# Turning the first rows inside the last group of a projection

## The chip, the cores and the metric

The kernel runs on one core of one Trainium2 chip. The metric is the device time of one execution in microseconds: three runs of the kernel before took 1815.97, 1819.52 and 1818.56 us, median 1818.56. Engines are called as the profile calls them: PE (matmuls), PEld (the loads of a matmul's stationary operand), DVE (vector), ACT (activations), POOL (GpSimd), SP (its queue issues most DMAs).

## The reference

One step of a decoder layer, for two groups that share weights. The prompt group has 1024 rows of width 1024, the sample group 8 rows with a paged cache of 8192 positions each.

```python
# prompt rows xp, for each layer (there is one)
q, k, v, logf, u, z = mixer_inputs(rmsnorm(xp, g_mix), w_in, b_f, g_sgu_v)
xp = xp + merge_heads(fox_prompt(q, k, v, logf), sgu_prompt(u, z, w_s, b_s), g_att_out, g_sgu_out, w_o)
mk, mv = memory_kv(mem_prompt, g_mem, w_ck, w_cv)
xp = xp + cross_attend(rmsnorm(xp, g_cross), mk, mv, w_cq, w_co)   # (softmax(q mk / 16) mv) @ w_co, 4 heads
f, conv = conv_ffn(rmsnorm(xp, g_ffn), zeros, w_up, conv_w, conv_b, w_down)  # silu(gate) * val, conv of width 3
xp = xp + f
# the sample rows go through the same layer, attending to cache_k[page_table], cache_v[page_table], cache_logf[page_table]
# a last rmsnorm follows for both; k, v, logf, mk, mv and the last conv rows are returned too
```

All is float32. Each prompt matmul is made of three: both operands are split in a high part (rounded by ACT) and a low part (the rest, by DVE), and high x high, high x low and low x high are summed.

## The kernel before

**The two streams.** The main stream, `prompt`, works on two halves of 512 rows, as four row tiles of 128 (called 0 to 3). Per half: `merge` of the two head groups, `out_proj` with w_o, `cross`, `out_proj` with w_co at the end of `cross`, and `ffn`. The second stream, `sample`, handles the sample rows: `decode` goes through the cache in steps, of which each gathers a tile of keys (1 MB, a 128x2048 tile, through POOL's queue), multiplies it on DVE (L1423) and sums it on DVE (L1427), and gathers values that go through PE (L1475); later `sample_rest` takes all weights through PE again for eight rows.

**The order.** Both streams are Python generators that yield a cost. The loop at the end of `build` adds the main stream's yields to a credit, and while the credit is at least `PACE` of the phase (8.0 in the first half's middle part, 6.8 in the second's, 8.5 in the first feed-forward, 2.5 in the second, 2.9 once the sample stream is in its rest) it emits a step of the sample stream, at most one or a few per yield. Nothing is emitted while `held[0]` is true; the credit goes on growing. This gives the order of the program; a scheduler then places the instructions on every engine's queue by its own simulated times, an earlier instruction going first where several are ready. [...] Decode's DVE instructions are put behind the newest DVE instruction of the main stream.

**The projections.** `out_proj` computes [512 rows] x [1024 columns] in two halves of the columns. In the first half (L1055 to L1057) all four row tiles go side by side. In the second half (L1073 to L1075) row tiles go in three groups, (0), (1) and (2, 3). A group has eight slices of the contraction, with three matmuls of 512 columns per slice and row tile: 24, 24 and 48. After a group `residual` adds the bank to x (L1007, DVE) and takes the square's sum (L230, ACT). Before a feed-forward, the rows are also scaled by their norm: `factor` (ACT L1023, then a power on POOL, L1024) and `scaled` (ACT L1029) for rows 0 and 1, `both` (L1036, L1037) for rows 2 and 3. Before `cross` this scale is applied later, in the softmax.

**The turn.** `norm_T` transposes the rows (L1106, PE) two row tiles at a time, four steps of two contraction slices each, and splits the result (L238 on ACT, L239 on DVE) into `hs` and `ls`. It then runs the first column tile of the next projection on these 256 columns of rows: 24 matmuls through `gemm3` (L272 to L274). So the first column tile is made in two halves, all others with 512 columns at once. This happens in four places: before `cross` and before `ffn`, in both halves.

**Buffers.** PSUM has four banks tagged `ba`, two `bb`, one `ms` and one `dv`; `BK` (also called `MM` and `TR`) takes `bb` at each third turn. Weights come by `wload`: a DMA into one of 4 `wr` buffers, then `split` into one of 5 `wh` (L235) and one of 4 `wl` (L236). `U` tiles (128x1024 floats, tag `u`) number 18, key and value tiles 4.

Of the kernel before, what the change touches and what calls it, by code (L numbers as in the profile page):

```python
# [30 lines left out]
NF = FF // P  # L31
# [47 lines left out]
def build(nc, tc, ctx, a, phases=None):  # L79
# [70 lines left out]
    MM = TR = BK  # L150
# [847 lines left out]
    held = [False]  # L998
# [15 lines left out]

    def out_proj(w, mh, ml, xt, fetch=None, ys=None):

        sq = squares()
# [9 lines left out]
        def scaled(i, r):  # L1027
            y = U([P, D])
            nc.scalar.activation(y, xt[i], AF.Copy, scale=r)  # L1029
            return y  # L1030
# [11 lines left out]
        for n in range(2):  # L1042
# [24 lines left out]
            for group in ((0,), (1,), (2, 3)):  # L1067
                pss = [MM() for _ in group]
                for k in korder:
                    wh, wl = (ws[k // 2][q][:, k % 2, :] for q in range(2))  # L1070
                    for i, ps in zip(group, pss):
                        tb = slice(i * P, (i + 1) * P)
                        mmul(ps, mh[k][:, tb], wh, start=(k == korder[0]), stop=False)  # L1073
                        mmul(ps, mh[k][:, tb], wl, start=False, stop=False)
# [14 lines left out]

    def norm_T(ys, g0, first):  # L1090


        hs, ls = [], []
        for t0 in (0, 2):
            c = slice(t0 * P, (t0 + 2) * P)
            if callable(ys[t0]):
                ys[t0:] = ys[t0]()
            for kk in range(0, 8, 2):
                if t0 == 0:
                    h2, l2 = U([P, 2, 512], F32R), U([P, 2, 512], F32R)  # L1100
                    hs += [h2[:, 0, :], h2[:, 1, :]]
                    ls += [l2[:, 0, :], l2[:, 1, :]]
                tr = TR()
                for q in range(2):
                    for i in range(2):
                        nc.tensor.transpose(  # L1106
                            tr[:, (q * 2 + i) * P : (q * 2 + i + 1) * P], ys[t0 + i][:, (kk + q) * P : (kk + q + 1) * P], ident
                        )
# [11 lines left out]
    def cross(xt, sq):  # L1120
        mkn, mkT, mv, pp, pT = ([None] * MH for _ in range(5))
# [10 lines left out]

        ws = [wload(wpair(a["w_cq"], kk, 0, 512), 1024) for kk in range(4)]
        q2, ps0 = [], MM()

# [108 lines left out]
        ys = []  # L1244
        sq = yield from out_proj(a["w_co"], oh, ol, xt, ys=ys)
        return ys


    hlast = [const.tile([P, 2 * NF, 2], F32, tag=f"hlast{h}", name=f"hlast{h}") for h in range(2)]

    def ffn(hf, xt, ys, late=None):
# [18 lines left out]
        for gi, gn in enumerate(GROUPS):  # L1270
            gh, gl = [], []
            for f in range(f0, f0 + gn):
                hc2 = []
                for part in range(2):
                    ft = f + part * NF
                    cw = [gp[:, CW + i * 44 + ft : CW + i * 44 + ft + 1] for i in range(3)]
                    cb = gp[:, CB + ft : CB + ft + 1]
                    if ft:
                        w_, pv = wload(a["w_up"][ft], 1024), BK()
                        up(pv, w_, hs, ls, slice(0, 512))  # L1280
                    else:
                        pv = pv0
                    hc = T2()
# [547 lines left out]
    def prompt():  # L1831
# [38 lines left out]
        for hf in range(2):  # L1870
# [8 lines left out]
            if ends:  # L1879
                yield from ends.pop()  # L1880
            sq = yield from out_proj(a["w_o"], mh, ml, xt, partial(load_x, hf))
            if hf == 0:
                ys = yield from mix(cross(xt, sq), gating(1), 0.05)
            else:
                ys = yield from cross(xt, sq)
            phase[0] = f"ffn{hf}"
            sq = yield from ffn(hf, xt, ys, (lambda: ahead.append(merge(*merge_in(1))) or ahead[0]) if hf == 0 else None)
            held[0] = False
# [123 lines left out]
```

## Time and profile before

| what | value |
|---|---|
| runs | 1815.97, 1819.52, 1818.56 us (median 1818.56) |
| profiled execution | 1820.56 us, of which the span of the program 1818.4 us |
| granted PE clock over the span | 0.986 |
| busy: PE / DVE / ACT / POOL | 1745.0 / 1397.5 / 734.4 / 510.0 us |
| moved by DMA | 521.06 MB, mean 287 GB/s |
| the four turns | 547.6 to 569, 706.6 to 727, 1182.6 to 1201, 1350.8 to 1364 us |

In the timeline a row has the start, the duration, engine, line, operation, the tiles written and read, the shape, and in brackets the idle time of the engine just before it with what ended it. Matmuls overlap, so what one costs is read from the distance of two starts, not from its duration. The granted clock is the share of full speed that PE had in a stretch.

### The profile page before, as it was taken

How to read it: one execution, taken by the hardware profiler on the slowest of the kernel's cores; microseconds unless marked ns; L12 is line 12 of the kernel's file. 1: busy time of each engine (PE TensorE's matmuls, PEld its weight loads, DVE VectorE, ACT ScalarE, POOL GpSimd, SP SyncE). 2: the span in 40 equal slices, each digit the busy share in tenths (PEclk: the TensorE clock that was granted, in tenths of full speed). 3: DMA queues.
4: the chain of work that ended last, by engine and by line, in shares of the span. 5: the costliest groups of instructions: out<-in, count | busy, mean ns of one | idle time of the engine just before them, and what ended most of it. 6: DMA issues, size and time to landing. Idle time of an engine off the chain costs nothing.

```text
span 1818.4 us, 25090 instructions
## 1 busy us (share of the span) xinstructions
PE 1745.0 (96%) x9637; PEld 1294.9 (71%) x9637; DVE 1397.5 (77%) x1729; ACT 734.4 (40%) x1378; POOL 510.0 (28%) x461
## 2 busy tenths in 40 slices
PE   8999999888998999999999999989899999999997
PEld 5887776656676767777777776766576778767775
DVE  4689668888788877999989899898875549845344
ACT  6332365455643544433333244235353324332332
POOL 1252334332133432223332333334222111011110
PEclk9999999899999999999999999989999999999999
DMA  8886889777696986679878779988787777568982
GB/s 295 306 297 231 302 297 329 242 266 224 219 398 257 342 310 260 257 285 340 316 279 311 271 306 340 381 300 324 290 309 290 267 268 265 179 266 289 359 314 82
DMA packets 157074, 521.06 MB, mean 287 GB/s; under 512 B 20874, under 2 KB 40842, under 8 KB 124186
## 3 DMA queue, kind: packets, MB, share of 16 engines
q0 software_dynamic: 57168, 341.14, 49.5%
q1 hardware_dynamic: 92874, 165.73, 26.4%
q10 hardware_dynamic: 6912, 12.59, 1.8%
q8 instruction: 76, 1.25, 0.3%
q14 instruction: 44, 0.36, 0.1%
HBM read 495.47 MB, written 23.93 MB: 286 GB/s over the span
## 4 chain that ended last, share of the span: by engine, by line
PE 72%; DMA 10%; issue 7%; DVE 6%; ACT 2%; POOL 2%; SPq 0%; POOLq 0%; DVEq 0%; ACTq 0%
PE ba L272 11%; PE ba L274 11%; PE ba L273 11%; PE bb L272 5%; PE bb L273 5%; PE bb L274 5%; PE dv L1475 5%; DMA kv<-cache_k,io 3%; DMA wr<-w_in 2%; DMA kv<-cache_v,io 1%; PE dv L321 1%; PE dv L1751 1%; PE ba L1056 1%; PE ba L1055 1%; PE ba L1057 1%
## 5 line engine op out<-in xcount | busy, mean ns | idle before, releaser
L235 ACT ACTIVATE wh<-wr 128x1024 fp32r<-128x1024 f32 (+2 forms) x220 | 228.9, 1044 | 489.2 <-PE ba L273 156.0
L236 DVE TENSOR_TENSOR wl<-wr,wh 128x1024 fp32r<-128x1024 f32 (+2 forms) x220 | 262.5, 1200 | 175.6 <-PE ba L274 65.7
L1407 POOL DMA_INDIRECT kv<-cache_k,io x128 | 205.6, 1606 | 551.2 <-DVE s L1427 318.9
L1423 DVE TENSOR_TENSOR kv<-kv,d 128x1024 f32<-128x1024 f32 (+1 forms) x156 | 258.0, 1681 | 35.1 <-DMA kv<-cache_k,io 35.1
L1427 DVE TENSOR_REDUCE s<-kv 128x16 f32<-128x1024 f32 (+1 forms) x156 | 258.2, 1674 | 0.1
L1469 POOL DMA_INDIRECT kv<-cache_v,io x128 | 165.3, 1291 | 282.8 <-PE dv L1475 191.8
L272 PE MATMUL ba<-u,wh 128*128 128x512 f32 (+1 forms) x560 | 220.3, 395 | 1.7 <-ACT u L238 1.7
L273 PE MATMUL ba<-u,wh 128*128 128x512 f32 (+1 forms) x560 | 220.2, 393 | 1.7 <-DVE u L239 1.5
L274 PE MATMUL ba<-u,wl 128*128 128x512 f32 (+1 forms) x560 | 219.5, 393 | 0.0
L272 PE MATMUL ba<-wh,u 128*128 128x512 f32 (+1 forms) x495 | 186.9, 379 | 0.9 <-ACT u L235 0.9
L273 PE MATMUL ba<-wl,u 128*128 128x512 f32 (+1 forms) x495 | 185.4, 375 | 1.2 <-DVE wl L236 1.2
L274 PE MATMUL ba<-wh,u 128*128 128x512 f32 (+1 forms) x495 | 183.8, 376 | 0.0
L272 PEld LDWEIGHTS ba<-u,wh 128*128 128x128 f32 x560 | 106.8, 191 | 30.6 <-issue 5.6
L273 PE MATMUL bb<-u,wh 128*128 128x512 f32 (+1 forms) x304 | 119.4, 393 | 9.2 <-DVE u L239 9.2
L274 PEld LDWEIGHTS ba<-u,wl 128*128 128x128 f32 x560 | 106.9, 191 | 29.1 <-issue 6.1
L273 PEld LDWEIGHTS ba<-u,wh 128*128 128x128 f32 x560 | 106.7, 191 | 27.5 <-issue 2.7
L1475 PE MATMUL dv<-kv,s 128*32 128x512 f32 x1024 | 124.2, 598 | 1.8 <-DMA kv<-cache_v,io 1.8
L272 PE MATMUL bb<-u,wh 128*128 128x512 f32 (+1 forms) x304 | 119.4, 393 | 0.0
L274 PE MATMUL bb<-u,wl 128*128 128x512 f32 (+1 forms) x304 | 118.6, 390 | 0.0
L272 PEld LDWEIGHTS ba<-wh,u 128*128 128x128 f32 x495 | 93.0, 188 | 26.0 <-issue 6.9
L274 PEld LDWEIGHTS ba<-wh,u 128*128 128x128 f32 x495 | 92.8, 188 | 21.5 <-issue 3.7
L273 PEld LDWEIGHTS ba<-wl,u 128*128 128x128 f32 x495 | 93.1, 188 | 19.7 <-DVE wl L236 1.9
(425 smaller groups left out, 3255.9 us busy)
## 6 DMA issues: line engine op xcount, KB each, us to landing
wr<-w_up SPq DMA_DIRECT2D x88, 512.0 KB
kv<-w_up POOLq DMA_DIRECT2D x22, 1024.0 KB, 8.0
wr<-w_down SPq DMA_DIRECT2D x40, 512.0 KB
kv<-w_down POOLq DMA_DIRECT2D x11, 1024.0 KB, 8.5
wr<-w_in SPq DMA_DIRECT2D x16, 512.0 KB
wr<-w_o SPq DMA_DIRECT2D x16, 512.0 KB
wr<-w_cq SPq DMA_DIRECT2D x16, 512.0 KB
wr<-w_co SPq DMA_DIRECT2D x16, 512.0 KB
```

Source lines behind the costliest of these rows:

```text
L235: nc.scalar.activation(h, src, AF.Copy)
L236: nc.vector.tensor_tensor(l, src, h.bitcast(F32), op=ALU.subtract)
L272: mmul(out, sh, mh, start=(i == 0), stop=False)
L273: mmul(out, sh, ml, start=False, stop=False)
L274: mmul(out, sl, mh, start=False, stop=(i == n - 1))
L321: mmul(ps[32 * j : 32 * j + 32, :w], xT[:, k, :] if nk == 8 else xT[:, k * 8 : k * 8 + 32], raw[:, q, j * w : (j + 1) * w], start=(k == 0) ...
L1055: mmul(pss[i], mh[k][:, tb], wh, start=(k == korder[0]), stop=False)
L1407: nc.gpsimd.indirect_dma_start(kv, None, a["cache_k"], off(kidx[:, b, ch : ch + 1]))
L1423: nc.vector.tensor_tensor(kvv[:, i : i + m, :], kvv[:, i : i + m, :], qb.unsqueeze(1).broadcast_to((P, m, 512)), op=ALU.mult)
L1427: nc.vector.tensor_reduce(s[:, ch * 4 + i : ch * 4 + i + m, :].rearrange("p k h -> p (k h)"), kvv[:, i : i + m, :].rearrange("p k (h d) -> ...
L1469: nc.gpsimd.indirect_dma_start(kv, None, a["cache_v"], off(kidx[:, b, ch : ch + 1]))
L1475: mmul(dv[32 * j : 32 * j + 32, :], s[:, ch * 4 : ch * 4 + 4, :].rearrange("p k h -> p (k h)"), kvv[:, j, :], start=(ch == 1), stop=(ch == ...
```

## The change

The transposes of rows 0 and 1 move into the last group of `out_proj`, the one of row tiles 2 and 3. `norm_T` now returns a generator `turn` with the two lists; `ahead_of` makes `hooks` from it, a table from slice number to what is to be emitted behind that slice: the loads of the weights of the next projection behind slices 0-based 1, 3, 5 (and 7 for the four w_cq loads), and the four steps of `turn(0)` behind slices 2, 3, 5, 6 before `cross` and 3, 4, 5, 6 before `ffn`. Row 1's scaling is emitted behind slice 1 of the group, where it was emitted behind the group.

`halves` follows the group: three banks of `ba` are taken, three column tiles run on columns 0 to 255 (rows 0 and 1), then `turn(2)` transposes rows 2 and 3, then the three tiles run on columns 256 to 511. In `cross` these are column tiles 0, 1, 2 of w_cq; in `ffn` the tiles 0, 22 and 1 of w_up. The loops that follow take these banks instead of computing the tiles.

`held[0]` becomes true at the start of the last group, where it became true at its end, and stays so until `halves` is done. The group's two banks, and those of the transposes of rows 2 and 3, are `bb`; the transposes of rows 0 and 1 use `ba`.

```diff
@@ out_proj, second half of the columns
             for group in ((0,), (1,), (2, 3)):
-                pss = [MM() for _ in group]
-                for k in korder:
+                held[0] = len(group) == 2
+                pss = [BB() if held[0] else MM() for _ in group]
+                for at, k in enumerate(korder):
...
-                    if len(group) == 2 and k == korder[3]:
-                        yield 5.2
-                if ys is not None and group[0]:
-                    ys.append(scaled(group[0] - 1, factor(group[0] - 1)))
+                    if len(group) == 2:
+                        if ys is not None and at == 1:
+                            ys.append(scaled(1, factor(1)))
+                        for hook in hooks.get(at, ()):
+                            hook()
+                        if at == 3:
+                            yield 5.2
+                if ys is not None and group[0] == 1:
+                    ys.append(scaled(0, factor(0)))
                 for i, ps in zip(group, pss):
                     residual(xt, sq, i, n, ps)
-
-                held[0] = len(group) == 2
                 yield 5.2
@@ norm_T: the body of the loop over rows becomes turn(t0)
-                tr = TR()
+                tr = BB() if t0 else BA()
...
-            first(hs, ls, c)
-            if t0 == 0:
-                yield 3
+
+        return hs, ls, turn
+
+    def ahead_of(turn, loads, at):
+
+        steps = turn(0)
+        hooks = {k: [partial(next, steps)] for k in at}
+        ws = []
+        for n, load in enumerate(loads):
+            hooks.setdefault(1 + 2 * n, []).insert(0, lambda load=load: ws.append(load()))
+        return hooks, ws
+
+    def halves(products, turn):
+
+        banks_ = [BA() for _ in range(3)]
+        for c in (slice(0, 256), slice(256, 512)):
+            if c.start:
+                for t in turn(2):
+                    yield t
+            for d, ps in enumerate(banks_):
+                products(ps[:, c], d, c)
+                yield 2.8
         held[0] = False
-        return hs, ls
+        return banks_
@@ cross
-        ws = [wload(wpair(a["w_cq"], kk, 0, 512), 1024) for kk in range(4)]
-        q2, ps0 = [], MM()
+        q2 = []
...
-        hs, ls = yield from norm_T(xt, G_CROSS, lambda hs, ls, c: products(ps0[:, c], ws, 0, hs, ls, c))
+        begun = yield from halves(lambda out, d, c: products(out, ws, d, hs, ls, c), turn)
...
-                if n or dt_:
+                if n or dt_ > 2:
...
-                    ps = ps0
+                    ps = begun[dt_]
...
+        hs, ls, turn = norm_T(ys, G_FFN)
+        hooks, ws = ahead_of(turn, [partial(wload, a["w_up"][ft], 1024) for ft in (0, NF, 1)], (3, 4, 5, 6))
+        yield from out_proj(a["w_co"], oh, ol, xt, hooks, ys=ys)
+        return hs, ls, turn, ws
@@ ffn
-        w0, pv0 = wload(a["w_up"][0], 1024), BK()
...
-        hs, ls = yield from norm_T(ys, G_FFN, lambda hs, ls, c: up(pv0[:, c], w0, hs, ls, c))
+        begun = yield from halves(lambda out, d, c: up(out, ws[d], hs, ls, c), turn)
+        begun = dict(zip((0, NF, 1), begun))
...
-                    if ft:
+                    pv = begun.pop(ft, None)
+                    if pv is None:
                         w_, pv = wload(a["w_up"][ft], 1024), BK()
                         up(pv, w_, hs, ls, slice(0, 512))
-                    else:
-                        pv = pv0
@@ prompt
+            hs, ls, turn = norm_T(xt, G_CROSS)
+            hooks, ws = ahead_of(turn, [partial(lambda kk: wload(wpair(a["w_cq"], kk, 0, 512), 1024), kk) for kk in range(4)], (2, 3, 5, 6))
+            sq = yield from out_proj(a["w_o"], mh, ml, xt, hooks, partial(load_x, hf))
```

More of the change, by code (lines that the diff above doesn't have):

```diff
@@ L1088, in out_proj, with norm_T, turn @@
         return sq
-    def norm_T(ys, g0, first):
+    def norm_T(ys, g0):
         hs, ls = [], []
-        for t0 in (0, 2):
+        def turn(t0):
             c = slice(t0 * P, (t0 + 2) * P)
@@ L1100, in norm_T @@
                     h2, l2 = U([P, 2, 512], F32R), U([P, 2, 512], F32R)
[L1101 to L1103 removed]
+                    hs.extend([h2[:, 0, :], h2[:, 1, :]])
+                    ls.extend([l2[:, 0, :], l2[:, 1, :]])
+                tr = BB() if t0 else BA()
                 for q in range(2):
@@ L1112, in norm_T, with cross @@
                 yield 0.6
-            first(hs, ls, c)
-            if t0 == 0:
-                yield 3
+        return hs, ls, turn
[15 more added lines that the diff above has]
+                yield 2.8
         held[0] = False
-        return hs, ls
-    def cross(xt, sq):
+        return banks_
+    def cross(xt, sq, hs, ls, turn, ws):
         mkn, mkT, mv, pp, pT = ([None] * MH for _ in range(5))
@@ L1244, in cross, with ffn @@
         ys = []
-        sq = yield from out_proj(a["w_co"], oh, ol, xt, ys=ys)
-        return ys
+        hs, ls, turn = norm_T(ys, G_FFN)
+        hooks, ws = ahead_of(turn, [partial(wload, a["w_up"][ft], 1024) for ft in (0, NF, 1)], (3, 4, 5, 6))
+        yield from out_proj(a["w_co"], oh, ol, xt, hooks, ys=ys)
+        return hs, ls, turn, ws
     hlast = [const.tile([P, 2 * NF, 2], F32, tag=f"hlast{h}", name=f"hlast{h}") for h in range(2)]
-    def ffn(hf, xt, ys, late=None):
-        w0, pv0 = wload(a["w_up"][0], 1024), BK()
+    def ffn(hf, xt, hs, ls, turn, ws, late=None):
         def up(out, w, hs, ls, c):
@@ L1880, in prompt @@
                 yield from ends.pop()
[L1881 to L1885, printed above, removed]
+            hs, ls, turn = norm_T(xt, G_CROSS)
+            hooks, ws = ahead_of(turn, [partial(lambda kk: wload(wpair(a["w_cq"], kk, 0, 512), 1024), kk) for kk in range(4)], (2, 3, 5, 6))
+            sq = yield from out_proj(a["w_o"], mh, ml, xt, hooks, partial(load_x, hf))
+            step = cross(xt, sq, hs, ls, turn, ws)
+            got_ = yield from (step if hf else mix(step, gating(1), 0.05))
             phase[0] = f"ffn{hf}"
-            sq = yield from ffn(hf, xt, ys, (lambda: ahead.append(merge(*merge_in(1))) or ahead[0]) if hf == 0 else None)
+            sq = yield from ffn(hf, xt, *got_, (lambda: ahead.append(merge(*merge_in(1))) or ahead[0]) if hf == 0 else None)
             held[0] = False
```

2 lines of the change are left out of this document (1 added, 1 removed).

## The prediction

> **What bounds the kernel now.** I read the page first, then the stages around the four projection ends, then single engines there.
>
> ```profile
> span 1818.4 us, 25090 instructions
> ...
> PE 1745.0 (96%) x9637; PEld 1294.9 (71%) x9637; DVE 1397.5 (77%) x1729; ACT 734.4 (40%) x1378; POOL 510.0 (28%) x461
> ...
> PE 72%; DMA 10%; issue 7%; DVE 6%; ACT 2%; POOL 2%; SPq 0%; POOLq 0%; DVEq 0%; ACTq 0%
> ```
>
> PE is busy 96% of the span and carries 72% of the chain: time comes only from PE's gaps and its clock. The stages, four of them the places that the diff touches (columns: window, length, busy of PE, PEld, DVE, ACT, POOL, granted clock, DMA share, GB/s):
>
> ```profile
> 548.00:570.00 22.00, 18.82 (x114) 15.20 (x113) 21.20 (x34) 9.38 (x22) 5.38 (x6) 0.84 0.87 330
> 707.00:725.00 18.00, 14.89 (x80) 12.51 (x79) 11.34 (x25) 12.39 (x31) 3.54 (x4) 0.81 0.81 329
> 1183.00:1203.00 20.00, 13.96 (x91) 10.86 (x94) 18.44 (x30) 9.40 (x21) 6.82 (x5) 0.74 0.77 273
> 1351.00:1366.00 15.00, 13.38 (x83) 11.87 (x82) 10.08 (x21) 11.81 (x29) 1.10 (x2) 0.89 0.42 165
> 570.00:590.00 20.00, 18.35 (x104) 13.21 (x106) 13.37 (x19) 6.18 (x8) 8.68 (x3) 1.00 0.51 178
> 725.00:800.00 75.00, 75.00 (x355) 57.16 (x355) 71.62 (x70) 30.46 (x49) 19.50 (x14) 1.00 0.64 237
> 800.00:1100.00 300.00, 300.00 (x1418) 222.36 (x1417) 280.15 (x252) 103.15 (x155) 95.22 (x65) 1.00 0.82 310
> 1250.00:1285.00 35.00, 28.87 (x128) 19.89 (x124) 27.74 (x31) 19.89 (x54) 13.32 (x8) 0.95 0.83 297
> ```
>
> In the first four PE idles and the clock falls; in 725 to 1100 PE never idles. Inside the places (timeline; the last bracket is idle time and its releaser):
>
> ```profile
> 546.20 0.39 PE L1073 MATMUL ba<-wh,u 128*128 128x512 f32 x1
> 546.43 0.39 PE L1074 MATMUL ba<-wl,u 128*128 128x512 f32 x1
> 547.59 1.03 PE L1106 MATMUL ba<-cp,u 128*128 128x128 f32 x8
> 548.46 0.60 PE L1106 MATMUL bb<-cp,u 128*128 128x128 f32 x4
> 552.13 0.28 PE L272 MATMUL bb<-u,wh 128*128 128x256 f32 x1
> 552.25 0.28 PE L273 MATMUL bb<-u,wh 128*128 128x256 f32 x1
> 560.14 0.39 PE L273 MATMUL bb<-u,wh 128*128 128x256 f32 x1 [2.05 <-DVE u L239]
> 563.98 0.58 PE L273 MATMUL bb<-u,wh 128*128 128x256 f32 x1 [0.80 <-DVE u L239]
> 712.01 0.47 PE L1106 MATMUL ba<-cp,u 128*128 128x128 f32 x1 [1.12 <-ACT u L1036]
> 712.98 0.58 PE L272 MATMUL ba<-u,wh 128*128 128x256 f32 x1 [0.50 <-ACT u L238]
> 1193.97 0.58 PE L273 MATMUL bb<-u,wh 128*128 128x256 f32 x1 [5.59 <-DVE u L239]
> 1199.88 0.28 PE L274 MATMUL bb<-u,wl 128*128 128x256 f32 x1
> 1355.29 0.39 PE L272 MATMUL ba<-u,wh 128*128 128x256 f32 x1 [1.04 <-ACT u L238]
> ```
>
> Starts give the real cost of one: 0.23 us for 512 columns, 0.12 for 256, 0.87/8 = 0.109 for a transpose. The gaps wait for the split of transposed rows (L238, L239), and at 1193 DVE was busy elsewhere:
>
> ```profile
> 1191.18 2.35 DVE L1423 TENSOR_TENSOR kv<-kv,d 128x1024 f32<-128x1024 f32 x2
> 1193.44 0.47 DVE L239 SCALAR_TENSOR_TENSOR u<-ba,gp,u 128x256 fp32r<-128x256 f32 x1
> ```
>
> Decode's steps sit ahead of the prompt's split. That is what the earlier hold acts on.
>
> **The prize.** Idle: 3.18 + 3.11 + 6.04 + 1.62 = 13.95 us. Clock: (1 - granted) x length = 3.52 + 3.42 + 5.20 + 1.65 = 13.8. Idle inside slow time is counted twice: in the third place 10.4 us (twice 5.20) ran slow (0.58 at 1193.97), up to the return to 0.28 at 1199.88, so it began near 1189.4 and about 4.5 us of the gap lay in it: 2.2 too many. Half of the 0.80 in the first and of some 1.4 in the second make 1.1 more. 27.7 - 3.3 = **24.4 us** is the most that can go. Since PE has no spare time behind the places, what is saved there reaches the end.
>
> **The change, part by part.**
>
> *Rows 0 and 1 turned inside the last group.* 16 transposes (1.7 us of PE, as before) move between the slices of the 48 matmuls of rows 2 and 3 (48 x 0.23 = 11 us), so their eight splits run under these. Are the rows there? Before a feed-forward, row 1 must pass residual, square, POOL's power and scaling:
>
> ```profile
> 1340.86 0.68 DVE L1007 TENSOR_TENSOR u<-ba,u 128x512 f32<-128x512 f32 x1
> 1344.11 1.16 ACT L1029 ACTIVATE u<-u,fac 128x1024 f32<-128x1024 f32 x1 [0.68 <-POOL fac L1024]
> ```
>
> That takes 4.4 us; the first hook stands behind 4 x 6 x 0.23 = 5.5 us. Covered by 1.1; without it PE, in program order there, would stand for the difference. Cross needs only the residual. PE cost 0.
>
> *Three tiles begun on columns 0 to 255.* 72 half products (8.6 us) stand where 24 stood, so the residuals, scaling and transposes of rows 2 and 3 are hidden by 8.6 instead of 2.9 us. Price: 48 more pairs of halves per place, each 2 x 0.12 - 0.23 = 0.01: 192 x 0.01 = **1.9 us**. [...]
>
> *Rows 2 and 3 turned behind the 72,* in the two BB banks alone. Nothing covers the first split:
>
> ```profile
> 706.65 0.60 PE L1106 MATMUL bb<-cp,u 128*128 128x128 f32 x4
> 707.87 0.36 PE L272 MATMUL ba<-u,wh 128*128 128x256 f32 x1
> 707.28 0.47 ACT L238 ACTIVATE u<-bb,gp 128x256 fp32r<-128x256 f32 x1 [2.14 <-PE bb L1106]
> ```
>
> From transpose to first product 1.22 us, of which eight transposes fill 0.87; the low part (DVE, 0.47 at 1193.44) costs some 0.4 more. 0.8 per place, **3.2 us**. Ends: 0 if the order pulls the transposes forward; 6.5 if each place stays as the best one was (1.62).
>
> *Weights.* The four w_cq or three w_up loads (SP's DMA, ACT's high and DVE's low part) move into the group, in the same order on SP; the four key and value fetches of cross now queue behind the w_cq loads, and are first read after five column tiles (27 us of PE at 24 x 0.23 each). The last w_cq slice's buffer comes free only at the group's end: two residuals (0.68 each) and its low part (wl, 1.22 below) make 2.6 us, wanted after 18 half products, 2.2. **0.9 us** for two cross places; ends 0 and 2.4, where both low parts stand bare.
>
> *The hold.* Decode stops at the group's start: 29.6 units of yields are held (2 x 5.2, 6 x 2.8, 4 x 0.6) in place of 13.0 (5.2, 8 x 0.6, 3), some 32 us of PE work (11 + 3.5 + 144 x 0.12). Work held is not saved: 16.6 more units are owed afterwards, two steps per place, each of two DVE instructions over a 128x2048 tile, and POOL's gathers wait for buffers that these release. On PE decode's matmuls only move. A place's yields grow from 28.6 to 40.0 units in all, so over the whole kernel decode is asked for sooner, and its tail is no new end.
>
> ```profile
> 731.02 2.28 DVE L1423 TENSOR_TENSOR kv<-kv,d 128x2048 f32<-128x2048 f32 x1
> 733.22 1.22 DVE L236 TENSOR_TENSOR wl<-wr,wh 128x1024 fp32r<-128x1024 f32 x1
> 734.36 0.74 DVE L1286 SCALAR_TENSOR_TENSOR t<-ba,gp,t 128x511 f32<-128x511 f32 x1
> 735.02 2.28 DVE L1427 TENSOR_REDUCE s<-kv 128x32 f32<-128x2048 f32 x1
> ```
>
> In the first feed-forward three yields of finished tiles come at once, each with a step of 4.6 us: 13.7 us of DVE while PE has one ready tile, 5.5 us, and a pair of decode's matmuls, 1.9. Weight splits slip between (733.22), so I take **2.5 us**, between 0 and 6.3 (13.7 - 7.4).
>
> *Clock.* Left gaps of 0.8 us: does it still fall?
>
> ```profile
> 588.92 1.50 PE L1475 MATMUL dv<-kv,s 128*32 128x512 f32 x12 [1.65 <-DMA kv<-cache_v,io]
> ```
>
> A lone gap of 1.65 left 570 to 590 at 1.00; a cluster with none above 1.04 cost 1.65 us at 1351. I take one such loss in the four, **1.7**; ends 0 and 6.8. [...]
>
> **Sum.** 24.4 - 1.9 - 3.2 - 0.9 - 2.5 - 1.7 = **14.2 us**. The profiled execution took 1820.56 us (span 1818.4), 2.0 above the runs' median of 1818.56: 1806.4 for it, **1804.4** as a median. All good ends: 24.4 - 1.9 = 22.5, 1796.1. All bad ends: 24.4 - 1.9 - 6.5 - 2.4 - 6.3 - 6.8 = 0.5, 1818.1.
>
> **Rivals.**
>
> *The transposes do not get under the group.* They wait for rows, for banks (BA, four) or for the 18 U buffers (8 for the turned rows, 8 for the projection's input, 4 for x). Then only the wait for rows 2 and 3 is hidden, about half the prize: 12.2 - 1.9 - 3.2 - 2.5 = 4.6, 1814.0. For: the margin of 1.1. Against: each slice frees two U buffers before a hook wants them. Chance 0.13.
>
> *DVE becomes the bound after the release.* In the first feed-forward a tile wants 1.22 + 2 x 0.74 + 0.68 = 3.4 us of DVE, a step 4.6: 8.0 against 6.5 to 7.4 on PE, for 29.6 / (8.5 - 5.2) = 9 tiles. 1.5 x 9 = 13 us if all shows: the gain is 14.2 + 2.5 - 13 = 3.7, 1815. For: DVE is 95% busy (71.62 of 75). Against: the same catch-up over four tiles there cost PE nothing. Chance 0.11.
>
> *Slower: late keys block DVE's queue.* A step released into a full DMA waits at DVE's head with the prompt's splits behind it:
>
> ```profile
> 1275.38 2.36 DVE L1423 TENSOR_TENSOR kv<-kv,d 128x1024 f32<-128x1024 f32 x2 [4.81 <-DMA kv<-cache_k,io]
> 1278.40 2.08 PE L1170 MATMUL bb<-t,u 128*128 128x256 f32 x4 [4.19 <-DVE u L236]
> ```
>
> That cost 4.19 and 0.05 x 35 = 1.75 of clock, 5.9. From the third such new stall on (14.2 / 5.9 = 2.4) the change loses; four make 1828. For: after the hold a step comes every 5.2 units where 6.8 or 8.0 were paced, 2 MB of keys and values in some 5.5 us, 380 GB/s, above the 297 in which this one waited. Against: four key buffers fill during the hold, and 570 to 590 has half the DMA free. Chance 0.16.
>
> **How the numbers follow.** The forecast has 0.60: 1804.4, its own range from the good ends to half of the bad ones, 1796 to 1811. Faster takes the forecast, the first rival and a quarter of the second: 0.76; within 0.2% (3.6 us, about what this kernel's measurement can tell) 0.08; slower 0.16. The range 1795 to 1823 reaches through the second rival into the third.
>
> **What would show it.** Transposes between slices of the last group, their splits done by its end; four windows with clock above 0.95 and under 1.5 us idle; 256-column products three times as many; DVE without decode in them, and in the first feed-forward PE idle below 3 us. It is wrong if the clock still falls in these places, or if new gaps ended by DMA or DVE stand in the 40 us behind a release.

## The result, and the profile after

The changed kernel takes 1828.32 us (median of 9 runs, 1821.75 to 1835.07), the kernel before 1816.06 (9 runs, 1811.78 to 1819.52). The ratio is 1.0061 [1.0044, 1.0078]: about 12 us slower, where 14 us faster was forecast.

The page of the changed kernel, first lines and the chain that ended last:

```profile
span 1821.4 us, 25458 instructions
...
PE 1744.1 (96%) x9829; PEld 1301.8 (71%) x9829; DVE 1397.6 (77%) x1725; ACT 736.3 (40%) x1378; POOL 517.3 (28%) x461
...
PE 41%; issue 15%; DMA 11%; DVE 8%; POOL 5%; ACT 1%; POOLq 0%; DVEq 0%; SPq 0%; ACTq 0%
```

PE is as busy as before (96%), but it carries 41% of the chain instead of 72%; DMA, DVE and POOL, the engines of decode's steps, carry 24% instead of 18%. The stages (columns as in the prediction: window, length, busy of PE, PEld, DVE, ACT, POOL, granted clock, DMA share, GB/s); the first four are the places, the others lie behind them:

```profile
548.00:570.00 22.00, 21.46 (x177) 19.42 (x176) 21.73 (x37) 7.31 (x16) 9.41 (x6) 1.00 0.89 355
707.00:729.00 22.00, 18.63 (x140) 17.89 (x139) 8.76 (x18) 11.26 (x26) 1.08 (x2) 0.92 0.31 108
1202.00:1222.00 20.00, 17.86 (x149) 15.77 (x148) 19.64 (x28) 5.72 (x12) 7.11 (x6) 1.00 0.95 351
1357.00:1375.00 18.00, 17.97 (x147) 17.37 (x146) 6.85 (x14) 9.63 (x21) 1.10 (x2) 1.00 0.43 177
615.00:630.00 15.00, 11.80 (x53) 7.09 (x52) 12.87 (x16) 7.01 (x19) 4.89 (x4) 0.77 1.03 402
...
800.00:900.00 100.00, 99.02 (x472) 72.43 (x472) 92.04 (x80) 34.87 (x52) 41.01 (x23) 1.00 0.86 318
925.00:945.00 20.00, 16.34 (x61) 12.81 (x60) 16.63 (x17) 5.17 (x5) 4.07 (x3) 0.83 0.78 290
1100.00:1151.00 51.00, 45.12 (x227) 31.69 (x226) 45.13 (x52) 19.80 (x37) 17.36 (x16) 1.00 0.98 382
1545.00:1562.00 17.00, 13.59 (x48) 10.57 (x47) 17.00 (x22) 5.36 (x9) 2.16 (x3) 0.80 0.65 219
```

The places are mended: idle there is 0.54 + 3.37 + 2.14 + 0.03 = 6.1 us for 13.95 before, and the clock costs 0.08 x 22 = 1.8 us for 13.8. But in stretches where PE hardly idled before it now waits, with the clock down behind it: 615 to 630, 925 to 945 and 1545 to 1562. From 1100 to 1151 it idles 5.9 us at full clock, in five waits of at most 1.8 us.

What PE waits for (timeline, PE; the last bracket is idle time and its releaser). The first two rows are transposes between slices of the last group, as planned; the row at 707.21 has the 12 transposes that came behind their group; the others are the waits:

```profile
546.32 0.49 PE L1110 MATMUL ba<-cp,u 128*128 128x128 f32 x3
547.81 0.60 PE L1110 MATMUL ba<-cp,u 128*128 128x128 f32 x4
...
620.80 3.64 PE L1497 MATMUL dv<-kv,s 128*32 128x512 f32 x16 [3.20 <-DMA kv<-cache_v,io]
707.21 1.47 PE L1110 MATMUL ba<-cp,u 128*128 128x128 f32 x12
711.92 0.42 PE L272 MATMUL ba<-u,wh 128*128 128x256 f32 x1 [3.25 <-DVE u L239]
933.60 0.39 PE L1482 MATMUL ms<-dg,ones 128*128 128x8 f32 x2 [2.32 <-DVE dg L1475]
935.33 0.80 PE L272 MATMUL ba<-wh,u 128*128 128x512 f32 x1 [1.34 <-DVE u L1341]
1556.18 0.80 PE L274 MATMUL ba<-wh,u 128*128 128x512 f32 x1 [3.41 <-DVE u L236]
```

At 933 and 1556 PE waits for something short on DVE. DVE's own order shows why: at 933 a multiply of decode's keys waits for its gather, and the 0.21 us instruction that PE wants (decode's own softmax), and the prompt's residual sums, stand behind it:

```profile
928.93 2.29 DVE L1445 TENSOR_TENSOR kv<-kv,d 128x2048 f32<-128x2048 f32 x1 [3.37 <-DMA kv<-cache_k,io]
931.14 2.28 DVE L1449 TENSOR_REDUCE s<-kv 128x32 f32<-128x2048 f32 x1
933.34 0.21 DVE L1475 TENSOR_SCALAR dg<-cp,mT 8x8 f32<-8x8 f32 x1
933.47 1.21 DVE L236 TENSOR_TENSOR wl<-wr,wh 128x1024 fp32r<-128x1024 f32 x1
934.60 1.27 DVE L1341 TENSOR_TENSOR u<-ba,u 128x512 f32<-128x512 f32 x2
```

DVE took these in that order: decode's 0.21 us and the prompt's sums, for which PE waits at 933 and at 935, stood 3.37 + 2.29 + 2.28 us behind a key step of decode. At 1556 DVE waits for no transfer at all; it is full with the sample's key steps, two products and two sums of 1.2 us each, ahead of the split (0.68 us) of the last gate product:

```profile
1547.32 2.35 DVE L1679 TENSOR_TENSOR kv<-kv,d 128x1024 f32<-128x1024 f32 x2
...
1552.06 2.33 DVE L1681 TENSOR_REDUCE sS<-kv 128x4 f32<-128x1024 f32 x2
1554.31 1.21 DVE L236 TENSOR_TENSOR wl<-wr,wh 128x1024 fp32r<-128x1024 f32 x1
1555.44 0.68 DVE L236 TENSOR_TENSOR u<-t,u 128x512 fp32r<-128x512 f32 x1
```

By stage (us between starts of matmuls in the trace; the last three columns are experiments told below):

| stage | before | after | after, second profile | turn | credit and turn | and sample |
|---|---|---|---|---|---|---|
| up to the end of w_o, first half | 546.9 | 548.9 | 550.8 | 547.7 | 550.0 | 549.0 |
| place 1, cross-attention, up to w_co | 104.9 | 104.0 | 107.4 | 101.6 | 100.8 | 98.8 |
| w_co | 54.1 | 53.6 | 53.6 | 53.7 | 53.8 | 53.8 |
| place 2, first feed-forward, merge, up to w_o | 429.3 | 444.7 | 446.5 | 441.4 | 427.5 | 426.0 |
| w_o, second half | 46.6 | 49.8 | 49.8 | 50.3 | 50.3 | 50.3 |
| place 3, cross-attention, up to w_co | 113.6 | 97.9 | 97.2 | 97.3 | 102.3 | 103.7 |
| w_co | 54.6 | 58.0 | 58.0 | 55.8 | 56.1 | 56.4 |
| place 4, second feed-forward, to the last matmul | 458.6 | 454.5 | 455.1 | 460.9 | 463.4 | 454.1 |
| last matmul starts at | 1808.7 | 1811.4 | 1818.3 | 1808.7 | 1804.1 | 1792.1 |

(The stages named w_o and w_co now hold the transposes of rows 0 and 1, so some 2 us move into them.) Up to the second half's w_co the gain comes in one stage, place 3, and goes in one, the first feed-forward, 15 us longer. (What place 1 gains, 0.9 us, is less than the 2 us that moved out of it.) Of the 15.7 us at place 3, 3.2 moved into w_o, and some 6 belong to the late key at 1278 that the prediction shows in the kernel before (4.19 us of idle and 1.75 of clock): neither profile of the changed kernel has that wait, and no term of the sum had it. In the first feed-forward the gaps grew from 5.8 to 17.0 us, the slow clock cost 1.7 more, and three key steps more, with 16 value matmuls of 0.12 us, brought 1.9: 14.7 of the 15.4. The profiled execution of before took 4.5 us more than the median of its runs, that of after 5 us less than its; the second profile of after (1830.11 us) stands near its median, and its last matmul starts 9.6 us behind that of before.

### The profile page after: what moved, and what is told of

It reads as the page before. It is cut to its first block, busy times and chain, and to the rows that moved or that the text cites. A ratio compares the mean times of both kernels' runs of the same rounds, so it can differ in the third digit from the quotient of the medians.

```text
span 1821.4 us, 25458 instructions
## 1 busy us (share of the span) xinstructions
PE 1744.1 (96%) x9829; PEld 1301.8 (71%) x9829; DVE 1397.6 (77%) x1725; ACT 736.3 (40%) x1378; POOL 517.3 (28%) x461
## 4 chain that ended last, share of the span: by engine, by line
PE 41%; issue 15%; DMA 11%; DVE 8%; POOL 5%; ACT 1%; POOLq 0%; DVEq 0%; SPq 0%; ACTq 0%
DMA kv<-cache_k,io 5%; PE ba L273 5%; PE ba L274 5%; PE ba L272 5%; PE dv L1497 3%; POOL kv L1429 2%; PE bb L273 2%; PE bb L272 2%; DMA kv<-cache_v,io 2%; PE bb L274 2%; POOL kv L1491 2%; DVE s L1449 2%; DVE kv L1445 1%; DMA u<-an_d 1%; PE dv L321 1%
## 5 line engine op out<-in xcount | busy, mean ns | idle before, releaser
L1491 POOL DMA_INDIRECT kv<-cache_v,io x128 | 178.3, 1393 | 282.0 <-PE dv L1497 198.0
L273 PE MATMUL ba<-u,wh 128*128 128x512 f32 (+1 forms) x656 | 237.6, 366 | 1.4 <-DVE u L239 1.4
L274 PE MATMUL ba<-u,wl 128*128 128x512 f32 (+1 forms) x656 | 236.2, 363 | 0.0
L272 PE MATMUL ba<-u,wh 128*128 128x512 f32 (+1 forms) x656 | 232.0, 364 | 3.4 <-DVE u L239 3.2
L272 PE MATMUL ba<-wh,u 128*128 128x512 f32 (+1 forms) x521 | 199.4, 384 | 3.2 <-DVE u L1341 1.3
L273 PE MATMUL ba<-wl,u 128*128 128x512 f32 (+1 forms) x521 | 197.7, 381 | 2.0 <-DVE wl L236 2.0
L274 PE MATMUL ba<-wh,u 128*128 128x512 f32 (+1 forms) x521 | 194.4, 380 | 4.4 <-DVE u L236 4.4
L273 PEld LDWEIGHTS ba<-u,wh 128*128 128x128 f32 x656 | 123.9, 189 | 32.6 <-issue 9.0
L274 PEld LDWEIGHTS ba<-u,wl 128*128 128x128 f32 x656 | 123.9, 189 | 27.1 <-issue 7.3
L272 PEld LDWEIGHTS ba<-u,wh 128*128 128x128 f32 x656 | 121.3, 189 | 26.7 <-issue 3.5
L272 PEld LDWEIGHTS ba<-wh,u 128*128 128x128 f32 x521 | 99.4, 191 | 29.1 <-issue 5.7
L274 PEld LDWEIGHTS ba<-wh,u 128*128 128x128 f32 x521 | 98.9, 190 | 26.0 <-DVE u L236 5.3
L272 PE MATMUL bb<-u,wh 128*128 128x512 f32 x272 | 108.1, 397 | 0.0
L273 PE MATMUL bb<-u,wh 128*128 128x512 f32 x272 | 107.5, 395 | 0.0
L274 PE MATMUL bb<-u,wl 128*128 128x512 f32 x272 | 107.5, 396 | 0.0
```

What stands on the lines that cost most here:

```text
L272: mmul(out, sh, mh, start=(i == 0), stop=False)
L273: mmul(out, sh, ml, start=False, stop=False)
L274: mmul(out, sl, mh, start=False, stop=(i == n - 1))
L1491: nc.gpsimd.indirect_dma_start(kv, None, a["cache_v"], off(kidx[:, b, ch : ch + 1]))
```

## The experiments

**Decode's steps or the hold.** The first two theories: more of decode's steps fall into the first feed-forward (44 key steps for 41), or the earlier hold itself costs. Four kernels: the change with decode at a slower pace there (41 steps again), before at a faster one (45 steps), the change with the hold where it was, and before with the earlier hold alone.

```diff
-'ffn0': 8.5
+'ffn0': 9.1        # e5_pace91, on the changed kernel
+'ffn0': 7.7        # e6_before_pace77, on the kernel before
```

> The changed kernel with the pace of the first feed-forward at 9.1 instead of 8.5: nothing else. By count of the program, decode then does 41 key steps between w_co's last residual and the feed-forward's end, as the kernel before, where the changed kernel does 44. Theory A (the change pushes three more decode steps, some 14 us of DVE, into a feed-forward in which DVE is already full): that stage falls from 445 us to 425 to 430 and the whole to 1806 to 1814, clearly below the changed kernel's 1828. Theory B (the longer hold itself, by late transfers behind it): stage 440 or more, whole 1823 to 1830.

Measured: 1821.25 us, 1.0028 [1.0009, 1.0048]. Its first feed-forward took 434.6 us, 10 less than the changed kernel's, yet only 7 us came back in all.

> The kernel before with the pace of the first feed-forward at 7.7 instead of 8.5, which makes 45 key steps there of 41 and leaves everything else. Theory A: the stage grows from 429 us to 443 to 450; the second half's middle part gets shorter by some 5, since decode is done sooner; whole 1820 to 1830. Theory B: the stage stays within 4 of 429, whole 1812 to 1819.

Measured: 1813.96 us, 0.9995 [0.9977, 1.0013]. 45 steps cost the kernel before nothing, so the count of steps by itself is not what costs.

```diff
 # e2_late_hold, on the changed kernel
-                held[0] = len(group) == 2          (ahead of the group)
...
+                held[0] = len(group) == 2          (behind its residuals, as before)
```

> The changed kernel with the hold at the end of the last group again (the banks stay bb): 43 key steps in the first feed-forward. Theory A: nearly the changed kernel, 1820 to 1828, the stage 437 to 445. Theory B: most of the loss goes, 1808 to 1817.

Measured: 1828.33 us, 1.0046 [1.0025, 1.0066]: no better.

> The kernel before with the hold from the start of the last group and nothing else: 43 key steps in the first feed-forward of 41, no extra yields. Theory A: two steps more, 9 us of DVE there, part of it seen: 1816 to 1824. Theory B: the whole loss without any of the gain, 1828 to 1840.

Measured: 1816.89 us, 0.9999 [0.9986, 1.0013]. The earlier hold by itself, on the kernel before, costs nothing and brings nothing.

**What the change is worth without the second stream.** Decode and sample left out of both kernels:

```diff
-    bgs.append(sample())
+    bgs.append(iter(()))
```

> The kernel before without the second stream: decode and all that follows for the sample rows behind the input projection is left out, so their outputs are not written. PE's prompt work alone. Base for the next run; 1560 to 1640 (1024 decode matmuls and the sample rows' weights less).

> The changed kernel without the second stream. With DVE free at the places the splits wait less, so the gain should be smaller than the 24 us of idle time and clock: theory C 6 to 16 us below the kernel before without the stream; theory D less than 4 below, or above.

Measured: 1584.63 us (1582.75 to 1586.93) and 1571.58 us (1569.89 to 1574.84). The change gains 13.1 us on the prompt alone. With the second stream it loses 12: some 25 us go in the meeting of the two streams. That 13.1 is near the 14.2 of the forecast is luck. The forecast rests on 24.4 us of idle and slow time in the places, and most of that is made by the second stream: without it the kernel before idles 5.1 us in them (22 us around each) and loses 3.4 to the clock, the changed kernel 0.6 and nothing. That is some 8 of the 13.1 us; where the other 5 come from is not shown.

```diff
 # n_one: n_after with one begun tile
-        banks_ = [BA() for _ in range(3)]
+        banks_ = [BA()]
...
-                if n or dt_ > 2:
+                if n or dt_ > 0:
...
```

> The changed kernel with one column tile begun on rows 0 and 1 instead of three, and without the second stream (the sample's outputs are not written). It stands against the two kernels without that stream, 1584.6 before and 1571.6 after. If the transposes in the group carry the gain: 1572 to 1575. If the three begun tiles do, by hiding the wait for rows 2 and 3: 1580 to 1585. The prediction's split, about half each: 1578.

Measured: 1588.5 us (1587.55 to 1592.35), 4 us above the kernel without the change. With one begun tile, rows 2 and 3 have too little work in front of them (their transposes wait 2.32 and 1.74 us for scaled rows before the two feed-forwards), and the transposes in the group bring nothing by themselves. The gain needs the three tiles; a split of about half each, as expected here, was wrong. One thing besides is not held in this run: it takes 11 fewer turns of the psum banks per place where n_after takes 13, and the turn matters, as told below.

**Late transfers.** Third theory: the gain is lost to gathers that come late. Decode's gathers cut to a quarter of their bytes in both kernels:

```diff
-            nc.gpsimd.indirect_dma_start(kv, None, a["cache_k"], off(kidx[:, b, ch : ch + 1]))
+            nc.gpsimd.indirect_dma_start(kv[:, :512], None, a["cache_k"].rearrange("r (q c) -> (r q) c", c=512), off(kidx[:, b, ch : ch + 1]))
...
```

> The kernel before with decode's gathers of keys and values cut to a quarter of their bytes (columns 0 to 511 of the tile); DVE multiplies the query by itself in place of the keys, into the same tile, and PE reads the first quarter four times, so every engine's work stays and the decode result is not the reference's. It is the base for the next run. Theory C (the change's gain is real at the four places and is spent on transfers that come late at other places, where they block PE or DVE in order): 1795 to 1812, since its own late transfers go too. Theory D (the new order of banks and slices itself costs PE time elsewhere): about the same.

> The changed kernel with the same quarter gathers. Theory C: 10 to 20 us below the kernel before with quarter gathers, no PE gap over 2 us before 1400 that a decode transfer ends; what remains of the loss lies behind 1400, where the sample rows' weight pages are as large as ever. Theory D: within 5 us of it or above, with the gaps at the same places (617, 930, 1120) as in the changed kernel.

Measured: 1832.48 us, 1.0089 [1.0068, 1.0111], and 1843.57 us, 1.0149 [1.0126, 1.0171]. q_before misses both theories, and q_after, above it as theory D has it, has its gaps at other places: with less to transfer both kernels became slower, and the change still costs 11 us. In the changed kernel a prompt split now came 8.88 us late (timeline, PE):

```profile
602.35 0.58 PE L273 MATMUL ba<-u,wh 128*128 128x256 f32 x1 [8.88 <-DVE u L239]
```

DVE was busy all that time: decode's steps, none of them waiting for a transfer, and weight splits stood ahead of it. The pair does not test lighter transfers alone. The order of the queues is written from simulated times, and with smaller gathers it was written anew: in q_before DVE has four of decode's products (8.90 us from 55.26 on) ahead of weight splits that come first in the kernel before, and PE waits 3.25 us for a split at 65.4. 10 of the 13 us by which q_before's last matmul is later lie ahead of the first place.

**A full DVE.** Fourth theory, from this row: DVE is the engine that has no room. The key step computes on a quarter of the tile in both kernels; and, as the reverse, the changed kernel's step is cut in two, so that short work can slip between.

```diff
 # v_before, v_after
-                        kvv[:, i : i + m, :], kvv[:, i : i + m, :], qb.unsqueeze(1)...
+                        kvv[:, i : i + m, :128], kvv[:, i : i + m, :128], qb[:, :128].unsqueeze(1)...
...
 # fine_after
-            sp = KS if phase[0][:3] == "mid" or held[0] else 1
+            sp = KS
```

> The kernel before, with decode's key step multiplying and summing a quarter of each gathered key tile (columns 0 to 127 of each row of 512) instead of all of it; the gathers themselves are whole. Decode's scores are therefore of 16 of each head's 64 columns. It is the base of the pair with the changed kernel. Vector-engine theory: the prompt's short splits wait behind decode's key steps, which fill that engine; with some 128 steps of 4.6 us cut to about 1.5 us, this kernel comes out 5 to 15 us under the kernel before. Late-gather theory: 0 to 5 us under it, since the waits for gathered keys and values stay.

> The changed kernel with the same quarter key step. Vector-engine theory: with that engine no longer full, the change keeps most of what it gains on the prompt alone (13.1 us without the second stream): 8 to 13 us under the base of this pair. Late-gather theory: the gathers are as large and as late as before, so the loss stays: 0 to 12 us above the base.

> The changed kernel with decode's key step cut into two multiplies and two sums of 1.2 us in the feed-forwards too, where it was one of 2.3 us each. Vector-engine theory: the prompt's short operations can slip in between, 1816 to 1825. Late-gather theory: no change, 1825 to 1831; the added instructions cost that engine some 0.1 us a step.

Measured: 1797.43 us, 0.9907 [0.9872, 0.9942]; 1818.53 us, 1.0009 [0.9994, 1.0024]; and 1838.49 us, 1.0123 [1.0094, 1.0151]. So the change costs 21 us where DVE is light, against the theory. Finer steps made the changed kernel 10 us slower, but that does not speak against it: the edit also cuts the 26 whole steps ahead of the first place, and there, up to the end of w_o, the kernel is 13.0 us longer (22.2 us of slow clock for 10.2), while its first feed-forward is 5.0 us shorter. One part held in the light pair too: the first feed-forward is 5.7 us shorter after the change (419.5 for 425.2), where it was 15 longer. But the cross-attention now waits for its own key rows, 12.6 and 10.8 us in the two halves (9.7 in all in the other kernel of the pair). Why they come so late is not shown; in this pair too the order of the queues was written anew. The second of them (timeline, PE, of v_after):

```profile
1272.32 1.11 PE L1175 MATMUL ba<-cp,t 128*128 128x128 f32 x4 [10.77 <-DMA t<-o_mk]
```

A new wait each time, at another place: whatever is taken away, the two streams are merged in another order and stop each other elsewhere. That led to the fifth theory.

**The order itself.** The change does two things beyond the places that its text does not show. It gives decode and sample other credit, so that their steps lie elsewhere among the prompt's tiles from then on; and since the group's last banks, the transposes and the begun tiles no longer draw from the turn that deals out psum banks (13 fewer draws a place; one draw in three is a BB), the tiles behind the first, second and fourth place get other banks (behind the third, 39 fewer is a whole number of threes). Both put back by two lines:

```diff
 # x_turn: the second hunk; x_credit_turn: both; x_same: both, and the hold as in e2_late_hold
-                yield 2.8
+                yield 0.9
...
         held[0] = False
+        turn_[0] += 13
         return banks_
```

> The changed kernel with the turn of the psum banks alone moved on by 13 at the end of each place, so that the tiles behind it get the banks that they had before. If the banks' turn is the cause: 1805 to 1815. If the second stream's order is: 1822 to 1832, as the changed kernel.

> The changed kernel, its hold from the group's start as it is, with the lower credit of 0.9 per half product and the banks' turn put back. Phase theory: 1804 to 1814, near the run with the late hold. Places theory: 1819 to 1830.

> The changed kernel with everything that the change shifts beyond the four places put back: the hold from the group's end, 0.9 instead of 2.8 units for each half product, so that decode is given the same credit as before (in program order its key steps then lie as before, 102 in front of the second half's projection instead of 105), and the turn of the psum banks moved on by 13, so that the column tiles behind a place get the banks that they had. Phase theory (the change gains at the places, and loses because the second stream and the banks meet the prompt's tiles elsewhere in another order): 1802 to 1811. Places theory (the new order inside the places itself goes ill with the second stream): 1819 to 1830.

> The changed kernel as it is, for a second profile of it. If its new stalls belong to the order that is written down, the same ones stand in both profiles (PE behind the value gather near 620, the sums near 930, the gate product near 1552), within 2 us each; if they belong to when transfers happen to land, other ones do, and the sum of idle and slow time differs by 5 us or more. Median 1824 to 1832 by both.

Measured beside a kernel before of 1816.99 us: the changed kernel again 1829.43 us, 1.0083 [1.0061, 1.0106]; with the banks' turn 1820.68, 1.0018 [1.0003, 1.0032]; with credit and turn 1815.41, 0.9999 [0.9975, 1.0023]; with the old hold as well 1818.07, 1.0021 [1.0008, 1.0034]. Turn and credit together bring back all of the loss: 8.7 us with the turn, clear of the noise, and 5.3 more with the credit, which by the intervals is not (they overlap; the credit alone was not run). x_credit_turn missed its 1804 to 1814 narrowly, and x_same its 1802 to 1811 clearly: the loss is gone, the gain is not there. How the turn acts is not shown. It moves more than banks: DVE's written order in x_turn differs from that of the changed kernel from about 573 us on.

The second profile of the changed kernel tells which waits are written into the order (timeline, PE, of again_after):

```profile
592.73 1.05 PE L1497 MATMUL dv<-kv,s 128*32 128x512 f32 x2 [3.68 <-DMA kv<-cache_v,io]
...
627.29 2.64 PE L1497 MATMUL dv<-kv,s 128*32 128x512 f32 x16 [2.44 <-DMA kv<-cache_v,io]
...
942.23 0.47 PE L1482 MATMUL ms<-dg,ones 128*128 128x8 f32 x2 [2.68 <-DVE dg L1475]
943.96 0.79 PE L272 MATMUL ba<-wh,u 128*128 128x512 f32 x1 [1.25 <-DVE u L1341]
...
1562.51 0.50 PE L274 MATMUL ba<-wh,u 128*128 128x512 f32 x1 [3.41 <-DVE u L236]
```

The wait of 3.41 us for the gate product stands there to the hundredth, those for the sums within 0.4 us, that for the values near 620 within 0.8. The one at 592 is new: value gathers come late now here, now there.

**The wait that is left.** Every changed kernel with the second stream and whole gathers waits between 1545 and 1570 for DVE, and the profiles say for what: the sample's key steps stand on DVE where a group of w_up tiles (an up-group) ends and the products with w_down want the last gate product. The sample's eight key steps are asked for 4 units apart instead of 3; in a second kernel decode's pace in the first feed-forward is 7.7 as well.

```diff
-CMK = 3
+CMK = 4            # x_sample4, on x_credit_turn
-'ffn0': 8.5
+'ffn0': 7.7        # x_sample4_pace77, besides
```

> The run with the lower credit and the banks' turn put back, and the sample's eight key steps of the second feed-forward asked for 4 units apart instead of 3. In the four profiles of changed kernels PE waits 3 to 7 us near 1552 for sums and splits that stand behind these steps on the vector engine, and the clock falls for 3 to 7 us behind it. If that written order makes the wait, most of it goes: 1809 to 1813, under the kernel before. If it was some transfer, no change: 1814 to 1817.

> The same with decode asked for every 7.7 instead of 8.5 units in the first feed-forward, which moves its steps against the prompt's tiles once more (106 key steps in front of the second half's projection instead of 102). On the kernel before this pace made no difference (0.9995). If the changed places leave that engine as much room as before: 1807 to 1813. If the room is gone there, as the changed kernel's own first feed-forward with 105 steps shows (444.7 us for 429.3): 1818 to 1826.

Measured: 1802.69 us (1800.71 to 1804.49), 0.9925 [0.9909, 0.9940], and 1808.50 us, 0.9957 [0.9942, 0.9972]. The stretch from 1535 to 1575, first in x_credit_turn:

```profile
1535.00:1575.00 40.00, 33.95 (x137) 25.39 (x137) 36.95 (x58) 11.58 (x18) 3.42 (x5) 0.96 0.61 219
```

and in x_sample4, with its four places ahead of it (the fourth begins at 1338; 1.00 us of idle at 1339.8 is not in its row) and the stretch around 930:

```profile
548.00:570.00 22.00, 21.46 (x177) 19.42 (x176) 21.73 (x36) 7.31 (x17) 9.46 (x6) 1.00 0.90 357
704.00:726.00 22.00, 21.76 (x174) 19.53 (x174) 10.68 (x20) 12.82 (x29) 3.93 (x5) 1.00 0.31 107
1180.00:1202.00 22.00, 19.83 (x147) 17.65 (x146) 18.51 (x27) 5.86 (x12) 9.47 (x7) 0.92 0.80 293
1345.00:1362.00 17.00, 16.76 (x144) 15.41 (x142) 5.54 (x11) 7.96 (x18) 0.54 (x1) 1.00 0.28 117
925.00:945.00 20.00, 20.00 (x92) 14.97 (x91) 17.74 (x18) 8.05 (x9) 7.27 (x3) 0.94 0.68 245
1535.00:1575.00 40.00, 40.00 (x175) 32.45 (x174) 37.68 (x47) 13.05 (x18) 3.42 (x5) 1.00 0.57 188
```

6.05 us of idle are gone in the last stretch and the clock stays at 1.00; the last stage shrinks by 9.3 us. The stages ahead of it shrink by 2.7 together, though DVE's order is the same in both kernels up to 1524, so of the 12.7 us between the medians 9.3 are shown to be the edit's. This kernel is 13.7 us faster than the one before: nearly what was forecast for the change, but with three corrections that the change did not have. What the other spacing would do to the kernel before was not run; its own stretch from 1535 to 1575 has 0.9 us of idle (39.08 busy of 40) and a clock of 1.00, so there is little to gain there.

The pace of 7.7, which cost the kernel before nothing, costs 5.8 us here: its time fell into the range of the first theory, but the price beside x_sample4 is real. Its first feed-forward takes 438.8 us for 426.0.

## Why the prediction was wrong

**The prize** (24.4 us) was there to be had in the places: their idle went from 13.95 to 6.1 us and the clock's cost from 13.8 to 1.8. What the sum did not see is that most of it is the second stream's work standing ahead of the prompt's splits (without that stream the places hold 8.5 us), and this work is still owed behind them.

**The price of the halves** (1.9 us) is a difference of rounded numbers. By the median distance of two starts in the changed kernel, 0.231 us for 512 columns and 0.118 for 256, a pair costs 0.005 more, 1.0 us in all.

**Rows 0 and 1 in the last group** came about in three places of four. Before the first feed-forward row 1's scaling ended 8.1 us behind its group (704.1), where 4.4 were reckoned and 5.5 allowed: a key step of decode stood ahead of its residual on DVE until 698.0. 12 of the 16 transposes stand behind the group (707.21), and PE waited 3.25 us for the first split: the first rival, at one place. That the transposes alone are worth nothing without the three tiles (n_one, 4 us above) the sum did not say; it took the two as parts that add up. The tiles without the transposes were not run.

**The first split of rows 2 and 3** at 0.8 us a place, 3.2 in all: 0.5 at the first place and 0.9 at the third in the changed kernel; 0.5, 0.2, 2.2 and 0.2 in x_sample4, 3.2 in all. **The clock's** one loss of 1.7: 1.8. Both terms held as sums, though not place by place.

**The hold** was priced 2.5 us in the first feed-forward. The hold itself costs nothing (0.9999). What failed is the sentence behind it: that a place's yields grow from 28.6 to 40.0 units, decode is asked for sooner over the whole kernel, and this needs no term. Put back to the old credit, the first feed-forward fell by 13.9 us and the whole by 5.3 (x_turn to x_credit_turn), the latter within the noise.

**The step that failed first** is the last sentence of the prize, that what is saved in the places reaches the end since PE has no spare time behind them. It takes the order behind the places as given. The order is written by credit and by a turn, and both moved. The banks' turn had no term in the sum at all: 8.7 us. The sample's steps at the end of an up-group in the second feed-forward had none either: 12.7 us between medians (x_credit_turn to x_sample4, 1815.4 to 1802.7), 9.3 in the stage itself. 8.7 + 5.3 + 12.7 = 26.7 us is about the distance from the forecast (1804.4) to the result (1828.3), but the parts were taken off one after the other, in one order, so this sum is no proof. x_same shows where the gain goes once hold, credit and turn are put back (one profile each): its last w_co product starts 15 us ahead of that of the kernel before (1335.5 for 1350.6), about the forecast, and the second feed-forward then takes 469.2 us for 458.6.

**The rivals.** The slower one named 5.9 us for a wait with its clock, four of them, and 1828 us. The profile has such a set: 3.20 us near 620, 2.32 + 1.34 near 933 and 3.41 at 1556, each with the clock down behind it (0.77, 0.83, 0.80), and a value gather 2.4 late at 1041. Its time was right, and at 933 its mechanism as it was described. Its cause was not: the burst behind a longer hold does not decide (e3_hold_only), nor do light gathers take the loss away (11 us between q_before and q_after), and at 1556 nothing is late. Its chance of 0.16 was too low, because the argument against it, that four buffers fill during the hold and the DMA has room, looked at the release and not at the order of everything that follows. The rival that DVE becomes the bound in the first feed-forward named 13 us; 11.1 us of new gaps came there. They go with a light key step (v_after), but also with the old credit and the full step (x_credit_turn, 427.5 us). DVE is busy 93% of that stage in x_credit_turn and 91% in the changed kernel, so its load alone does not make the gaps.

**Left open.** How the banks' turn acts; what the credit is worth alone; why the sample's steps meet the up-group's end as badly with hold, credit and turn put back (x_same idles 5.1 us from 1535 to 1575, the kernel before 0.9); and how much the spacing there would bring without the other two corrections.

## What to carry to other kernels

Where two streams are merged into one written order by credits, counters and turns, a local change has two prices: its own, and that of shifting every later step against the other stream. Measure the first without the other stream, hold the credits and turns constant to take the second out, and only then move the spacing at the one or two waits that both of two profiles show. Here a wait that recurred to the hundredth of a microsecond (1556) stood in the order and could be moved, and the one that came in one profile only (592) was a transfer. An experiment that changes the size of a step or a transfer changes the written order too, wherever a scheduler writes it from simulated times: compare the queues before reading the time.

## What the runs showed of the hardware

The same wait of 3.41 us cost different amounts of clock in two executions of the same kernel. The changed kernel's first profile has the clock at 0.80 in the 17 us around it (the row 1545.00:1562.00 above), 3.4 us lost; its second:

```profile
1551.00:1568.00 17.00, 13.59 (x53) 10.59 (x52) 17.00 (x22) 5.36 (x9) 2.16 (x3) 0.90 0.63 221
```

1.7 us lost. In the first profile the clock is 0.50 from 1556 to 1561. Products of 512 columns start 0.43 us apart there (from 1556.77 on), 0.23 ahead of the wait and again from 1562.21 on. In the second they start 0.23 apart behind the wait and 0.43 from 1563.89 on. At 0.50 the two losses are about 6.8 and 3.4 us of slow time, an estimate from the two granted clocks. Why one is twice the other is not shown.

Fewer bytes made both kernels slower (1832.48 for 1816.06 us with quarter gathers, 175 GB/s on average for 287). This is not the transfers' doing alone, since the order of the queues changed with them: in q_before the first of decode's products start on DVE at 55.26 us instead of 65.56, and weight splits stand behind them.
